# A decoder layer on one core: another timetable for the recurrence, and other memory for attention's first keys

## The chip, the core and the metric

One core of a Trainium2 chip. Its engines work beside each other, each through its own list of instructions in a fixed order: TensorE (PE; PEld is its weight load), VectorE (DVE), ScalarE (ACT), GpSimd (POOL), and SyncE (SP), which here issues the DMA transfers. They wait for each other by semaphores. The metric is the device time of one execution in microseconds, the median of several runs.

## The reference

One layer on x (1024 rows of 1024), all in float32. Cut to what matters:

```python
xn = rms_norm(x, norm_g)
z = xn @ w_in                       # q, c_kv, q_idx, k_idx, w_idx, g_attn, x_rnn, g_rnn, merge
s_idx = sum_j relu(q_idx_j @ k_idx.T) * w_idx_j        # index scores, causal
_, idx = lax.top_k(s_idx, 256)                         # for each row the 256 best keys
o = softmax(q_lat @ c_sel.T - slope * dist) @ c_sel    # attention over the chosen keys, 16 heads
y_attn = (o * silu(g_attn)) @ w_attn_proj
u = causal_depthwise_conv(x_rnn, conv_w, conv_b)
r, i = sigmoid(u_blocks @ w_a + b_a), sigmoid(u_blocks @ w_x + b_x)
a = exp(-8 * r * softplus(-lam))
h = scan(h * a + sqrt(1 - a*a) * (i * u))              # RG-LRU, along the sequence
y_rnn = (h * silu(g_rnn)) @ w_rnn_proj
g_a, g_r = split(sigmoid(merge + b_merge))
out = rms_norm(x + (g_a * y_attn + g_r * y_rnn) @ w_out, final_norm_gain)
```

## The kernel before

Each projection is made in three matmuls: both operands are split into a high and a low part (`split`, L94 to L96: the high part by ScalarE, the low part by GpSimd or VectorE), and three of the four products are added in PSUM (`proj_steps`, L116 to L124). A projection of 128 output columns for all 1024 rows is called a long piece here: 16 steps of three matmuls (L529: `step`), 512 rows wide each. Its weights come in two DMA transfers of 256 KB and are split one long piece ahead.

The stages are: normalisation and transposes; index scores; the stage of the timetable; attention with its projections; the output. The stage of the timetable holds three independent kinds of work:

- the recurrence, in four pairs of 128-channel groups c and d: input projections `xr` of c and d, convolution on VectorE (`conv`, L557 and L559), the split of its result (`both_parts`, ScalarE and GpSimd), gate projections `gr` of c and d with the small matmuls of the recurrence's gates between their steps (`gate_part`, L575 to L582); then the tail of the pair: `decay` (ScalarE), `radicand`, `root` and `scan` (VectorE), and the result is stored to DRAM (`u_r`, L608);
- the merge gates of the recurrence, `mr` 0 to 7, eight long pieces whose only consumer is the projection `rp` of the recurrence's result; then that projection, `rp` 4 to 7 and 0 to 3, whose result is multiplied by the gate on VectorE (L513) and stored (`mr_d`, L514);
- the choice of the 256 best keys, by a search for a threshold, bit by bit, 31 rounds. For the row blocks 2 to 5 (the near ones) a round is four counts and a step on VectorE (`near_round`, L633 to L647). For blocks 6 and 7 (the far ones) it is two sums of signs and a flag on ScalarE (`far_sums`, L656 to L660), and one small step on VectorE (`far_step`, L663: it writes `neg`, which the next round reads). After the rounds each block is selected in five steps (`select_at`, L729 to L742); for the far ones `far_last` (L684 to L691) comes before.

The order of all this is a timetable: every piece is entered with a time by `at_time`, the entries are sorted by it, and each engine's instructions are recorded in that order. So the times set the order alone; on the chip nothing waits for them. `STEP` is 0.68 for a step of a long piece, `LONG` 10.9.

After the pairs the recurrence's memory is closed (`close_rec`), the stored result is fetched in eight transfers of 512 KB (`fetch_u`, L759), and split (`part_u`: high part on ScalarE, low part on VectorE, for groups 2 and 5 on GpSimd), while the last merge gates run on TensorE. Then `rp` begins.

Attention opens a memory pool `at` where the stage's pools stood. A pool gives each tag its place when the first tile of it is asked for. In the kernel before the first are `vr` (the values' copy), `kh` and `kl` (keys), `qt` (queries); so `vr` stands on the memory of the products of `rp` (pool `grp`), and may be written once their stores to `mr_d` are done. The first key matmul's PSUM bank is that of the last projection's first half, which VectorE's product (L513) reads.

Of the kernel before, what the change touches and what calls it, by code (L numbers as in the profile page):

```python
# [8 lines left out]
F32 = mybir.dt.float32  # L9
F32R = mybir.dt.float32r  # L10
# [8 lines left out]
P = 128  # L19
S = 1024  # L20
# [32 lines left out]
def hybrid_kernel(ctx: ExitStack, tc: tile.TileContext, x, w_b, w_a, w_ap, w_rp, w_o, vecs,  # L53
# [98 lines left out]
    with ExitStack() as p12:  # L152
# [41 lines left out]
        with tc.tile_pool(name="xprep", bufs=3) as xp:  # L194
# [14 lines left out]
            for i in range(NB):  # L209
# [6 lines left out]
                if i < 2 or i % 2 == 0:  # L216
                    n = 1 if i < 2 else 2
# [168 lines left out]
        with tc.manual_schedule(engines={mybir.EngineType.PE}):  # L386
# [6 lines left out]
            for g in range(NG):  # L393
# [10 lines left out]
                for j in (2 * g, 2 * g + 1):  # L404
                    for cost in score_steps(j):
                        debt += cost * pace
                        while debt > 0:
                            f = next(beside, None)
# [41 lines left out]
        def at_time(t, fn, *a):  # L450
            plan.append((t, len(plan), fn, a))
# [215 lines left out]
        def near_round(t, apart=0.0):  # L667
            k = bits["near"]
            bits["near"] -= 1
            for b in near:  # L670
                at_time(t, lambda b=b: count(b, thf[:, b - B0:b - B0 + 1], ALU.is_ge))
                t += apart or 0.18 + 0.00108 * P * (b + 1)
            at_time(t, near_step, k)
            return t + 1.0

        def far_round(t):
            at_time(t, far_sums, bits["far"])
            bits["far"] -= 1
            at_time(t + 3.3, far_step)
# [96 lines left out]
        t = 0.0  # L776
        for p in range(4):
            c, d = 2 * p, 2 * p + 1
            t0 = t
            if p:  # L780
                tail(t0, c - 2, c - 1)
                near_round(t0 + 0.8)
                far_round(t0 + 15.0)
            else:
                near_round(t0 + 17.5)
            at_time(t0 + 1.0, gate_weights, c)
            at_time(t0 + 12.5, gate_weights, d)
            t = long(t, "mr", p)
            t1 = long(t, "xr", c)
            t2 = long(t1, "xr", d)  # L790
            at_time(t1 + 0.8, conv, c)
            at_time(t1 + 6.0, both_parts, c)
            near_round(t1 + 6.1)
            far_round(t1 + 2.4)
            at_time(t2 + 0.8, conv, d)
            at_time(t2 + 6.0, both_parts, d)
            near_round(t2 + 6.1)
            t3 = long(t2, "gr", c, gate_parts(c), 4)
            near_round(t3 - 1.4)
            far_round(t3 - 2.0)  # L800
            t = long(t3, "gr", d, gate_parts(d), 4)
            near_round(t - 7.5)
            far_round(t - 3.4)

        t0 = t
        tail(t0, 6, 7)
        near_round(t0 + 0.8)
        for n in range(4, 8):
            t = long(t, "mr", n)
        at_time(t0 + 23.0, close_rec)  # L810
        for c in range(8):
            at_time(t0 + 24.0, fetch_u, c)
            at_time(t0 + 29.0 + 2.0 * c, part_u, c)
        for n in (4, 5, 6, 7, 0, 1, 2, 3):
            t = long(t, "rp", n)
            if n > 3:
                at_time(t + 1.0, again, n - 4)
        for u in (15.0, 20.0, 36.2):
            far_round(t0 + u)
        u = t0 + 45.0  # L820
        while bits["far"] >= 0:
            far_round(u)
            u += 4.4
        far_end = u
        near_round(t0 + 23.2)
        for u in (28.6, 36.6):
            near_round(t0 + u, 2.0)
        u = t0 + 45.5
        while bits["near"] >= 0:
            u = near_round(u)  # L830
        at_time(t0 + 55.0, distances)
# [3 lines left out]
        for b in near:  # L835
            u = select_at(u, b)
        u = max(u, far_end)
# [3 lines left out]
        for b in FAR_B:  # L841
            u = select_at(u, b)
# [21 lines left out]

        with ExitStack() as p2:
            at = p2.enter_context(tc.tile_pool(name="at", bufs=2))
            p2.enter_context(tc.manual_schedule(engines={mybir.EngineType.PE}))
            vts, vraw, qts, khs, kls, os_, sgs, ws = {}, {}, {}, {}, {}, {}, {}, {}

# [568 lines left out]
```

## Time and profile before

| | us |
|---|---|
| median of 3 runs | 1199.71 (1199.65 to 1200.52) |
| profiled execution | 1199.43 |
| its span, first to last instruction | 1197.6 |
| TensorE busy | 1147.1 (96%) |
| VectorE busy | 847.4 (71%) |
| ScalarE busy | 752.8 (63%) |
| GpSimd busy | 475.0 (40%) |

Busy shares are means over stages that are bound differently. The stage of the timetable runs from about 153 us (first input projection) to 543 us (first key matmul of attention). On TensorE its borders are: pair 0 with its merge gate before 200.9, the three other pairs until 390.6, four merge gates until 434.2, the projection `rp` until 538. TensorE has two clock levels, 1.2 and 2.4 GHz; the windows show the granted share of the higher one, as a mean. An idle time stands in brackets with what ended it; where several semaphores are waited for, the last by the profile is named.

### The profile page before, as it was taken

To read this page: it belongs to the slowest core of one execution; us is meant where nothing else is said; L and a number is where in the kernel's file an instruction comes from. 1 tells how busy PE (TensorE), PEld (TensorE's weight loads), DVE (VectorE), ACT (ScalarE), POOL (GpSimd) and SP (SyncE) were. 2 spreads that over 40 slices of the span, in tenths; PEclk is the share of its full clock that TensorE was granted. 3 is DMA by queue.
4 is the path that set the end of the run, shared out by engine and by line. 5 is a ranking of instruction groups with operands and counts; after the bars stand their busy time and mean duration, and the time that the engine had idled before them with its cause. 6 is when DMAs were issued, how large, how long until landed. Compare 5 with 4: busy or idle time off the path is not lost.

```text
span 1197.6 us, 16198 instructions
## 1 busy us (share of the span) xinstructions
PE 1147.1 (96%) x5528; PEld 957.1 (80%) x5528; DVE 847.4 (71%) x1740; ACT 752.8 (63%) x1444; POOL 475.0 (40%) x379
## 2 busy tenths in 40 slices
PE   6989999989998979999999999999999998999997
PEld 5978888768787857877888888888888877888886
DVE  6878587888888669986867676767667699533335
ACT  6457549778787865636877767776767677322211
POOL 4211145454656342243453534344434436363000
PEclk8989999989999998999999999999999999999999
DMA  5110221313131143322011111111010241453322
GB/s 207 51 36 19 71 67 45 105 36 115 36 110 36 71 183 113 114 99 69 11 45 42 49 52 42 45 37 63 28 64 27 89 158 36 165 187 127 96 86 114
DMA packets 44402, 94.19 MB, mean 79 GB/s; under 512 B 5280, under 2 KB 8864, under 8 KB 44320
## 3 DMA queue, kind: packets, MB, share of 16 engines
q1 hardware_dynamic: 44176, 92.89, 22.8%
q8 instruction: 44, 0.72, 0.3%
q14 instruction: 38, 0.31, 0.1%
q10 hardware_dynamic: 144, 0.26, 0.1%
HBM read 70.59 MB, written 22.54 MB: 78 GB/s over the span
## 4 chain that ended last, share of the span: by engine, by line
PE 49%; DVE 2%; ACT 1%; issue 1%; DMA 1%; POOL 1%; POOLq 0%; ACTq 0%; DVEq 0%
PE pT L1273 5%; PE o L1227 3%; PE l L1069 3%; PE l L1070 2%; PE f L113 2%; PE f L114 2%; PE z_q L122 2%; PE f L112 2%; PE z_q L124 2%; PE z_q L123 2%; PE z_g L122 2%; PE z_g L124 2%; PE z_g L123 2%; PE z_ap L124 2%; PE z_ap L123 2%; PE z_ap L122 2%
## 5 line engine op out<-in xcount | busy, mean ns | idle before, releaser
L1277 DVE TENSOR_TENSOR pp<-pT,pp 128x512 fp32r<-128x512 f32 (+1 forms) x160 | 100.8, 634 | 36.7 <-ACT pp L1276 35.2
L1276 ACT ACTIVATE pp<-pT 128x512 fp32r<-128x512 f32 (+1 forms) x160 | 87.9, 551 | 52.3 <-PE pT L1273 50.3
L633 DVE TENSOR_SCALAR_CACHE_REDUCE junk<-sc,thr 128x384 bf16<-128x384 f32 (+4 forms) x130 | 106.2, 817 | 3.2
L656 ACT ACTIVATE junk<-sc,neg 128x896 int8<-128x896 f32 (+1 forms) x62 | 67.9, 1095 | 30.1 <-DVE neg L663 28.8
L1227 PE MATMUL o<-pp,vt 128*128 128x512 f32 x160 | 66.9, 418 | 2.2 <-DVE o L1242 1.0
L1069 PE MATMUL l<-kh,qt 128*128 128x128 f32 (+2 forms) x192 | 64.7, 339 | 1.6 <-DVE m L1071 0.9
L1070 PE MATMUL l<-kl,qt 128*128 128x128 f32 (+2 forms) x192 | 65.5, 342 | 0.0
L1077 ACT ACTIVATE l<-l,m 128x128 f32<-128x128 f32 (+4 forms) x80 | 54.0, 675 | 16.7 <-DVE m L1071 16.4
L1082 POOL TENSOR_SCALAR sc<-sc,m 128x384 f32<-128x384 f32 (+1 forms) x32 | 25.8, 808 | 87.8 <-DVE m L1079 79.6
L123 PE MATMUL z_rp<-url,whi_rp 128*128 128x512 f32 x128 | 52.6, 411 | 6.7 <-POOL url L96 3.5
L1242 DVE TENSOR_TENSOR o<-o,o 64x256 f32<-64x256 f32 x128 | 53.4, 419 | 6.8 <-ACT o L1240 4.6
L378 ACT ACTIVATE r<-s 128x512 f32<-128x512 f32 (+1 forms) x80 | 39.8, 522 | 26.2 <-PE s L377 23.4
L122 PE MATMUL z_q<-xh,whi_q 128*128 128x512 f32 x128 | 53.7, 419 | 0.2 <-DVE kl L953 0.2
L1077 ACT ACTIVATE sc<-sc,m 128x384 f32<-128x384 f32 (+2 forms) x48 | 44.9, 935 | 13.5 <-DVE m L1071 12.0
L383 DVE SCALAR_TENSOR_TENSOR sc<-r,wi,sc 128x384 f32<-128x384 f32 (+5 forms) x42 | 40.6, 1000 | 18.0 <-ACT r L378 17.7
L124 PE MATMUL z_rp<-urh,wlo_rp 128*128 128x512 f32 x128 | 52.1, 407 | 0.9 <-POOL wlo_rp L96 0.9
L96 POOL TENSOR_TENSOR xs<-xc,xs 64x1024 fp32r<-64x1024 f32 x16 | 38.4, 2402 | 36.2 <-ACT xs L95 28.3
L122 PE MATMUL z_rp<-urh,whi_rp 128*128 128x512 f32 x128 | 51.9, 405 | 0.6 <-ACT whi_rp L95 0.6
L122 PE MATMUL z_gr<-xh,whi_gr 128*128 128x512 f32 x128 | 51.3, 401 | 0.0
L1273 PE MATMUL pT<-ident,sc 128*128 128x128 f32 x288 | 48.9, 272 | 2.6 <-DVE pp L1277 2.6
L123 PE MATMUL z_gr<-xl,whi_gr 128*128 128x512 f32 x128 | 51.1, 399 | 0.0
L124 PE MATMUL z_gr<-xh,wlo_gr 128*128 128x512 f32 x128 | 51.0, 398 | 0.0
(356 smaller groups left out, 3921.2 us busy)
## 6 DMA issues: line engine op xcount, KB each, us to landing
xt<-in_x_dram SPq DMA_DIRECT2D x8, 512.0 KB, 8.8
wraw_mr<-in_w_b_dram SPq DMA_DIRECT2D x16, 256.0 KB, 2.7
wraw_xr<-in_w_b_dram SPq DMA_DIRECT2D x16, 256.0 KB, 2.7
wraw_gr<-in_w_b_dram SPq DMA_DIRECT2D x16, 256.0 KB, 2.7
u_r<-ig SPq DMA_DIRECT2D x8, 512.0 KB, 2.7
url<-u_r SPq DMA_DIRECT2D x8, 512.0 KB, 7.5
wraw_rp<-in_w_rp_dram SPq DMA_DIRECT2D x16, 256.0 KB, 3.1
mr_d<-grm SPq DMA_DIRECT2D x16, 256.0 KB, 2.0
```

The lines of the kernel that those rows point to most:

```text
L122: nc.tensor.matmul(acc, wh, xh_, start=(k == 0), stop=False)
L123: nc.tensor.matmul(acc, wh, xl_, start=False, stop=False)
L124: nc.tensor.matmul(acc, wl, xh_, start=False, stop=(k == KT - 1))
L633: nc.vector.tensor_scalar(junk[:, :P * (b + 1)], SL(b), thr_, None, op0=op, op1=ALU.add, accum_out=cnt[:, b - B0:b - B0 + 1])
L656: nc.scalar.activation(junk2[:, :P * (b + 1)], SL(b), AF.Sign, bias=nf[:, j:j + 1], accum_out=sums[:, j:j + 1])
L1069: nc.tensor.matmul(acc[:, :n], q, kh[:, c0:c0 + n], start=True, stop=False)
L1070: nc.tensor.matmul(acc[:, :n], q, kl[:, c0:c0 + n], start=False, stop=True)
L1077: nc.scalar.activation(l[:, :L], l[:, :L], AF.Exp, scale=-1.0, bias=mi, accum_out=m[:, 2:3])
L1227: nc.tensor.matmul(ov, vt[:, 2 * jj, :], pp[:, :, 0:256], start=(jj == 0), stop=False)
L1273: nc.tensor.transpose(tp[:, k * P:(k + 1) * P], pr[u][:, j * P:(j + 1) * P], ident)
L1276: latest[:] = [nc.scalar.activation(pp[:, 0, :n], tp[:, :n], AF.Copy), nc.vector.tensor_tensor(out=pp[:, 1, :n], in0=tp[:, :n], in1=pp[:, ...
L1277: nc.vector.tensor_tensor(out=pp[:, 1, :n], in0=tp[:, :n], in1=pp[:, 0, :n].bitcast(F32), op=ALU.subtract)]
```

## The change

The timetable is changed, and the order in which attention's memory is handed out. The merge gate that opened a pair (`mr` p in pair p) now opens the next one: pair 0 has none, pairs 1 to 3 have `mr` 0 to 2, and behind the pairs there are five (`mr` 3 to 7) in place of four. A pair has three far rounds: the one at t3 - 2.0, between the two gate projections, is gone, and pair 0's first is new at 2.0. Behind the pairs there are five fixed far rounds in place of three, and then one every 4.4 from 53.0 on in place of 45.0; the fixed near rounds are five in place of four. The splits of the fetched result stand 2.7 apart from 31.0 on, in place of 2.0 from 29.0 on. Before attention's first tile is asked for, a tile of each of six tags (`pp`, `o`, and four buffers of logits) is asked for, so that these get the lowest places.

```diff
@@ timetable of a pair
             t0 = t
+            near_round(t0 + 0.8)
             if p:
                 tail(t0, c - 2, c - 1)
-                near_round(t0 + 0.8)
-                far_round(t0 + 15.0)
-            else:
-                near_round(t0 + 17.5)
+                t = long(t, "mr", p - 1)
+            far_round(t0 + (15.0 if p else 2.0))
...
-            t = long(t, "mr", p)
...
             near_round(t3 - 1.4)
-            far_round(t3 - 2.0)
@@ behind the pairs
-        for n in range(4, 8):
+        for n in range(3, 8):
             t = long(t, "mr", n)
...
-            at_time(t0 + 29.0 + 2.0 * c, part_u, c)
+            at_time(t0 + 31.0 + 2.7 * c, part_u, c)
...
-        for u in (15.0, 20.0, 36.2):
+        for u in (15.0, 20.0, 25.0, 38.0, 46.1):
             far_round(t0 + u)
-        u = t0 + 45.0
+        u = t0 + 53.0
         while bits["far"] >= 0:
...
@@ attention
             at = p2.enter_context(tc.tile_pool(name="at", bufs=2))
+            for tag, w, dt, bufs in (("pp", S, F32R, 3), ("o", S, F32, 1), ("l0", P, F32, 1), ("l1", 2 * P, F32, 1),
+                                     ("l3", 4 * P, F32, 1), ("l4", 5 * P, F32, 1)):
+                at.tile([P, w], dt, tag=tag, name=f"{tag}_", bufs=bufs)
```

The order on ScalarE in the last pair, from the gates of group c (`r`, `ig`, read from PSUM banks `rg`) over the gate projection's second half (`sg`) and the next weights (`whi_mr`) to the first gates of group d. Before:

```order
L579 ACTIVATE r_3245<-rg_1_512_3362,vec 64x512
L579 ACTIVATE ig_3246<-rg_1_512_3362,vec 64x512
L656 ACTIVATE junk_1517,sums<-sc,neg 128x896
L656 ACTIVATE junk_1517,sums<-sc,neg 128x1024
L659 ACTIVATE sgn<-sums,lims 128x1 x2
L660 ACTIVATE flip<-sgn 128x2
L489 ACTIVATE sg_3275<-z_gr_512_3339 128x512
L95 ACTIVATE whi_mr_0_3397<-wraw_mr_0_3395 128x512
L95 ACTIVATE whi_mr_512_3403<-wraw_mr_512_3401 128x512
L579 ACTIVATE r_3334<-rg_0_0_3426,vec 64x512
L579 ACTIVATE ig_3335<-rg_0_0_3426,vec 64x512
```

and now:

```order
L579 ACTIVATE r_3166<-rg_1_0_3269,vec 64x512
L579 ACTIVATE ig_3167<-rg_1_0_3269,vec 64x512
L579 ACTIVATE r_3166<-rg_1_512_3283,vec 64x512
L579 ACTIVATE ig_3167<-rg_1_512_3283,vec 64x512
L489 ACTIVATE sg_3196<-z_gr_512_3260 128x512
L95 ACTIVATE whi_mr_0_3313<-wraw_mr_0_3311 128x512
L95 ACTIVATE whi_mr_512_3319<-wraw_mr_512_3317 128x512
L579 ACTIVATE r_3255<-rg_0_0_3341,vec 64x512
L579 ACTIVATE ig_3256<-rg_0_0_3341,vec 64x512
```

The four rows of the far round (two sums, the sign, the flag) between the gates of c and the gates of d are gone.

The order of SyncE's DMA issues at the fetch: `u_r` is the store of the recurrence's result, `url` the fetch, `wraw` the weights of the next long pieces. Before:

```order
L100 DMA wraw_mr_0_3664<-in_w_b_dram 128x512
L100 DMA wraw_mr_512_3670<-in_w_b_dram 128x512
L608 DMA u_r_80<-ig_3335 128x1024
L759 DMA url<-u_r_73 128x1024
L759 DMA url<-u_r_74 128x1024
L759 DMA url<-u_r_75 128x1024
L759 DMA url<-u_r_76 128x1024
L759 DMA url<-u_r_77 128x1024
L759 DMA url<-u_r_78 128x1024
L759 DMA url<-u_r_79 128x1024
L759 DMA url<-u_r_80 128x1024
L100 DMA wraw_rp_0_3760<-in_w_rp_dram 128x512
```

and now:

```order
L608 DMA u_r_80<-ig_3256 128x1024
L759 DMA url<-u_r_73 128x1024
L759 DMA url<-u_r_74 128x1024
L759 DMA url<-u_r_75 128x1024
L759 DMA url<-u_r_76 128x1024
L759 DMA url<-u_r_77 128x1024
L759 DMA url<-u_r_78 128x1024
L759 DMA url<-u_r_79 128x1024
L759 DMA url<-u_r_80 128x1024
L100 DMA wraw_mr_0_3679<-in_w_b_dram 128x512
L100 DMA wraw_mr_512_3685<-in_w_b_dram 128x512
L100 DMA wraw_rp_0_3766<-in_w_rp_dram 128x512
```

The weights of the last merge gate stood ahead of the fetch and now stand behind it, in the place of the first weights of `rp`.

The order on VectorE at the end of the selection of block 5 (`eq` to `sc`), with the steps of the far rounds (`neg`) and the products (`grm`), up to the first row of `far_last` (`tf`). Before:

```order
L736 SCALAR_TENSOR_TENSOR eq_4293<-pre_4294,need_4144,eq_4293 128x768
L739 SCALAR_TENSOR_TENSOR eq_4293<-sc,thr,eq_4293 128x768
L742 SCALAR_TENSOR_TENSOR sc<-eq_4293,dist 128x768
L663 TENSOR_TENSOR neg<-neg,flip 128x2
L513 TENSOR_TENSOR grm_3970<-grm_3970,z_rp_512_4309 128x512
L663 TENSOR_TENSOR neg<-neg,flip 128x2
L684 TENSOR_SCALAR tf<-neg 128x2
```

and now:

```order
L736 SCALAR_TENSOR_TENSOR eq_4244<-pre_4245,need_4113,eq_4244 128x768
L739 SCALAR_TENSOR_TENSOR eq_4244<-sc,thr,eq_4244 128x768
L663 TENSOR_TENSOR neg<-neg,flip 128x2
L742 SCALAR_TENSOR_TENSOR sc<-eq_4244,dist 128x768
L513 TENSOR_TENSOR grm_3994<-grm_3994,z_rp_0_4261 128x512
L663 TENSOR_TENSOR neg<-neg,flip 128x2
L513 TENSOR_TENSOR grm_3994<-grm_3994,z_rp_512_4311 128x512
L663 TENSOR_TENSOR neg<-neg,flip 128x2 x2
L513 TENSOR_TENSOR grm_4091<-grm_4091,z_rp_0_4344 128x512
L684 TENSOR_SCALAR tf<-neg 128x2
```

Behind the last selection row (`sc<-eq`) two steps of far rounds stood, and now three, with one more just ahead of it; one product more stands in front of `far_last`.

## Rows read from the trace of the kernel before

**Rows 1.** The page's busy shares: engine, busy us, share, instructions.
```profile
PE 1147.1 (96%) x5528; PEld 957.1 (80%) x5528; DVE 847.4 (71%) x1740; ACT 752.8 (63%) x1444; POOL 475.0 (40%) x379
```
**Rows 2.** Windows by stage: length, busy us by engine, granted clock, DMA share, GB/s.
```profile
153.07:200.90 47.83, 47.67 (x210) 39.05 (x209) 40.06 (x71) 33.05 (x55) 26.23 (x17) 1.00 0.19 63
200.90:266.60 65.70, 61.45 (x257) 49.61 (x256) 53.52 (x79) 53.42 (x88) 34.35 (x20) 0.95 0.21 68
266.60:328.94 62.34, 60.07 (x257) 49.14 (x256) 52.90 (x74) 50.08 (x81) 34.38 (x20) 0.97 0.22 72
328.94:390.56 61.62, 58.47 (x258) 47.99 (x256) 52.24 (x70) 49.47 (x77) 34.39 (x20) 1.00 0.21 71
390.56:434.20 43.64, 43.64 (x193) 35.86 (x191) 28.79 (x46) 30.25 (x48) 11.60 (x7) 1.00 0.42 157
434.20:538.00 103.80, 95.62 (x387) 73.94 (x387) 95.16 (x165) 60.27 (x129) 36.71 (x27) 0.95 0.30 101
```
**Rows 3.** Waits of TensorE: total us, times, longest.
```profile
PE rg L575 <- POOL wlo_mr L96: 8.9, 3, 3.5
```
**Rows 4.** Timeline of ScalarE, third pair: start, us, engine, line; in brackets idle before.
```profile
379.40 1.04 ACT L656 ACTIVATE junk<-sc,neg 128x896 int8<-128x896 f32 x1
...
382.21 0.20 ACT L660 ACTIVATE flip<-sgn 128x2 int32<-128x2 f32 x1
```
**Rows 5.** Timeline of VectorE, end of the last pair.
```profile
393.90 0.69 DVE L490 TENSOR_TENSOR sg<-sg,z_gr 128x512 f32<-128x512 f32 x1 [1.87 <-ACT sg L489]
```
**Rows 6.** Timeline of VectorE, GpSimd and TensorE, pair 0.
```profile
164.85 0.81 DVE L557 TENSOR_SCALAR xc<-xr,vec 128x1024 f32<-128x1024 f32 x1 [3.49 <-ACT xr L482]
...
172.69 2.39 POOL L96 TENSOR_TENSOR xs<-xc,xs 64x1024 fp32r<-64x1024 f32 x1 [3.63 <-ACT xs L95]
...
178.91 0.39 PE L575 MATMUL rg<-xs,rgh 128*128 128x512 f32 x1
```
**Rows 7.** Timeline of SyncE's DMA issues, the fetch.
```profile
419.59 4.37 SPq L759 DMA_DIRECT2D url<-u_r  x8
424.38 13.35 SPq L100 DMA_DIRECT2D wraw_rp<-in_w_rp_dram  x4
```
**Rows 8.** Timeline of ScalarE and VectorE behind the fetch.
```profile
434.15 1.27 ACT L95 ACTIVATE whi_rp<-wraw_rp 128x512 fp32r<-128x512 f32 x2 [8.32 <-DMA wraw_rp<-in_w_rp_dram]
...
437.35 3.42 DVE L96 TENSOR_TENSOR url<-url,urh 128x1024 fp32r<-128x1024 f32 x1 [7.92 <-ACT urh L95]
```
**Rows 9.** Line 656 (far rounds) in 446 to 515: durations, starts, idle before.
```profile
L656 ACT ACTIVATE junk<-sc,neg x26: 1027/1096/1151, 446.1 to 512.0; 128x896 int8<-128x896 f32 x13, 128x1024 int8<-128x1024 f32 x13
...
  DVE neg L663: 20.4, 11
```
**Rows 10.** Timeline of VectorE, the last selections.
```profile
507.69 1.01 DVE L736 SCALAR_TENSOR_TENSOR eq<-pre,need,eq 128x768 f32<-128x768 f32 x1
...
510.67 0.15 DVE L663 TENSOR_TENSOR neg<-neg,flip 128x2 int32<-128x2 int32 x1
...
513.91 0.16 DVE L663 TENSOR_TENSOR neg<-neg,flip 128x2 int32<-128x2 int32 x1 [2.49 <-ACT flip L660]
...
526.63 2.01 DVE L736 SCALAR_TENSOR_TENSOR eq<-pre,need,eq 128x896 f32<-128x896 f32 x1
...
542.25 1.28 DVE L513 TENSOR_TENSOR grm<-grm,z_rp 128x512 f32<-128x512 f32 x2
```
**Rows 11.** Timeline of TensorE, start of attention.
```profile
542.99 0.50 PE L112 MATMUL k<-cnh,ukh 128*128 128x512 f32 x1 [2.11 <-DVE grm L513]
...
557.79 0.30 PE L1069 MATMUL l<-kh,qt 128*128 128x128 f32 x1 [0.63 <-PE z_q L124]
```
**Rows 12.** Timeline of ScalarE, start of attention.
```profile
547.22 2.07 ACT L919 ACTIVATE vr<-v 128x512 f32<-128x512 f32 x4 [0.33 <-DMA mr_d<-grm]
```
**Rows 13.** Timeline of GpSimd beside the selection of block 6.
```profile
523.07 4.61 POOL L96 TENSOR_TENSOR wlo_rp<-wraw_rp,whi_rp 128x512 fp32r<-128x512 f32 x2 [3.30 <-ACT whi_rp L95]
```
**Rows 14.** The page's costliest groups, line 633 (near counts).
```profile
L633 DVE TENSOR_SCALAR_CACHE_REDUCE junk<-sc,thr 128x384 bf16<-128x384 f32 (+4 forms) x130 | 106.2, 817 | 3.2
```

More of the change, by code (lines that the diff above doesn't have):

```diff
@@ L806, in hybrid_kernel @@
         tail(t0, 6, 7)
-        near_round(t0 + 0.8)
-        for n in range(4, 8):
+        for n in range(3, 8):
             t = long(t, "mr", n)
@@ L816, in hybrid_kernel @@
             if n > 3:
-                at_time(t + 1.0, again, n - 4)
-        for u in (15.0, 20.0, 36.2):
+                at_time(t + 3.0, again, n - 4)
+        for u in (15.0, 20.0, 25.0, 38.0, 46.1):
             far_round(t0 + u)
-        u = t0 + 45.0
+        u = t0 + 53.0
         while bits["far"] >= 0:
@@ L824, in hybrid_kernel @@
         far_end = u
+        near_round(t0 + 0.8)
         near_round(t0 + 23.2)
-        for u in (28.6, 36.6):
-            near_round(t0 + u, 2.0)
-        u = t0 + 45.5
+        for u in (31.5, 39.6, 47.7):
+            near_round(t0 + u, 1.95)
+        u = t0 + 55.8
         while bits["near"] >= 0:
```

## The prediction

> **What bounds the kernel now.** First the page's busy shares: TensorE works 96% of the span [rows 1], so a change pays only where TensorE stands still, or where its clock falls. Second the windows, cut at the stage borders that TensorE's own rows give [rows 2]. In the three stretches 200.90 to 390.56 (a pair each) TensorE idles 4.25, 2.27 and 3.15 us, and in 434.20 to 538.00 (the recurrence's projection) 8.18. The clock column says more: a mean clock of 0.95, 0.97 and 0.95 over 65.70, 62.34 and 103.80 us is a loss of 3.3, 1.9 and 5.2 us, since a stretch at 1.2 GHz does half the work. With the 2.11 us in front of the first key matmul [rows 11] the idle is 20.0 and the clock loss some 12 with what follows that wait. Third the list of waits: the stalls in the pairs are the gate matmuls' [rows 3], put down to GpSimd, but GpSimd had long been done. In the third pair ScalarE runs a far round from 379.40 to 382.41 [rows 4] ahead of the copies that free the gates' PSUM banks, and only then can TensorE go on. Fourth VectorE: in 434.20 to 538.00 it is busy 95.16 of 103.80 us [rows 2], from 513.91 on it works through the last two selections and the last products until 542.9 [rows 10], and the first key matmul waits for its last product [rows 11]. So TensorE and VectorE reach attention nearly together, and what is saved on TensorE alone stops at VectorE.
>
> **The change, part by part.** I follow VectorE, since its last product releases the keys.
>
> *Pair 0 without its merge gate.* Four gates are the 192 matmuls of the window from 390.56, 43.64 us, so one is 10.9 [rows 2]. TensorE passes it on to the tail, where the total is the same. VectorE's first convolution waited 3.49 us for the recurrence's input, until 164.85 [rows 6]; that input is now made a gate earlier, so the wait goes. ScalarE's first far round (3.0 us, as in rows 4) now stands before the copy and takes about 0.5 back: VectorE gains 3.0. TensorE arrives much earlier and meets a new wait: in before the GpSimd split for the first gate matmul ended 10.2 us after the convolution began (172.69 + 2.39 - 164.85 [rows 6]); the convolution now begins at about 161.9, so the split is there at 172.1, and TensorE at 178.91 - 10.9 = 168.0: a wait of 4.1, and some 2 of lost clock, as after the 2.27 us wait [rows 2]. It costs the end nothing as long as VectorE comes later than TensorE.
>
> *One far round fewer in each pair.* The round of rows 4 goes, 3.0 us of ScalarE, four times. TensorE's waits of 3.45, 2.27 and 3.15 shrink to about 0.4, 0 and 0.1. VectorE waits for ScalarE at the pair's end (1.87 [rows 5]) and in the tail of the recurrence. It gains between 1.87 and 3.0 a pair; I take 2.5. Its busy time in the three later pairs is 53.52, 52.90 and 52.24 [rows 2], its idle time in an ordinary one 9.4; with 6.9 they last 60.4, 59.8 and 59.1, together 179.3 against 189.7: 10.4 earlier. Pair 0 gives 3.0 + 2.5. VectorE is then 15.9 us earlier at the end of the pairs.
>
> *Five gates beside the fetch.* The recurrence's result is fetched in eight transfers from 419.59; the next weights are issued behind them at 424.38 [rows 7] and ScalarE waits 8.32 us for them, until 434.15; VectorE waits 7.92 us behind ScalarE [rows 8]. TensorE's 8.18 us come from there. Now a gate's weights stand in that place, and TensorE has one gate more to do before it needs the splits. So most of the 8.18, and the 5.2 of clock, go. ScalarE and VectorE, however, wait just as before. What is late next is the order behind the wait. VectorE has two counts more there (2 x 0.82 [rows 14]), one split more (between 0 and the 3.42 of rows 8; I take half, 1.7), one product less (0.64), and the wait ends 1.0 sooner, as one 128x1024 copy less stands in front: +1.7.
>
> *Three far rounds more behind the pairs.* From 446.1 to 513.9 thirteen rounds took 67.8 us, 5.2 each; ScalarE needs 3.0 and waited 20.4 us for VectorE in that time [rows 9], so as long as VectorE has other work, a further round is hidden. It is not hidden after the fourth near block's selection. There the order shows one flag that is waited for before and three now; each costs 513.91 - 510.67 = 3.24 [rows 10], and between the last two ScalarE also splits a pair of weights (1.27, as in rows 8). The first runs beside one more selection step (1.01 [rows 10]). 3 x 3.24 + 1.27 - 1.01 = 10.0 against 3.24: +6.8. Bounds: 0, if ScalarE gets ahead in time; 15.6, if each of three costs the full 5.2.
>
> *The last two selections.* The weights of the last projection are issued earlier against the last flag, since the product in front of them moved ahead. The selection step at 526.63 took 2.01 for 896 columns, the one at 507.69 took 1.01 for 768 [rows 10], and beside the slow one GpSimd split weights from 523.07 to 527.68 [rows 13]. The Trainium skill (SBUF — State Buffer, section "Who interferes with whom") has it that a VectorE instruction with two SBUF inputs and a GpSimd instruction that reads SBUF block each other for the whole instruction; these rows agree. By that rule the doubling moves with the splits rather than with the selection, and all six slow steps could lose it, or other work could gain it. From the rows alone: two steps lose 1.0 each: -2.0, with 0 and -5.5 as bounds (five or six slowed steps of about 1.0).
>
> *Attention's first keys in other memory.* The values' copy stood on the memory of the products and waited for their stores (547.22, released by mr_d [rows 12]); the changed order of allocation puts it on the fetched result's memory, which the last projection matmul frees. On TensorE this wait is worth no more than the 0.63 us before the first logits at 557.79 [rows 11], because 48 query matmuls (10.9 us) lie beside it. -0.6. If it added a wait instead, the same 10.9 us would hide it.
>
> *Sum.* VectorE's last product, and with it the first key matmul, comes 15.9 - 1.7 - 6.8 + 2.0 = 9.4 us earlier. TensorE, with its waits and lost clock gone (20.0 + 12, less 6 new in pair 0 and the 1.9 behind the key matmul's own wait), would be there 24 us earlier, so for some 15 us in all it waits there and for the last projections' weights, which are issued behind the stores of products. A longer wait costs more clock: after the wait of 2.11 it was about as much as the 1.9 of the second window; I take 3.3 as in the first [rows 2], +1.4, less 0.6 for the keys: +0.8. Profiled execution: 1199.43 - 9.4 + 0.8 = 1190.8 (the span of 1197.6 and the 1.8 around it, which does not change). The median of the runs is 0.28 above that execution: 1191.1.
>
> **The rivals.**
> 1. *TensorE sets the pace.* VectorE and the far chain keep up, because VectorE's idle time in the pairs (9.4 to 12.2 each) is enough to take in everything. Then all 20.0 of idle and 12 of clock go, less 6 new in pair 0: 1199.7 - 26 = 1173.5, and what lies between that and my forecast. For it: no single row shows VectorE out of reach. Against it: 95.16 of 103.80 busy, and three serial flags.
> 2. *No change.* VectorE's waits in the pairs stay at 9.4 each (only the longer first one falls to that): 186.8 instead of 189.7 in three pairs, 2.9, and 3.0 in pair 0. Then 5.9 - 8.5 + 2.0 = -0.6, and 1199.43 + 0.6 + 0.8 + 0.28 = 1201.1. For it: the other waits there are for ScalarE's chain behind a table load, which does not change.
> 3. *Slower: VectorE's order paces both stages.* Pairs as in 2, and the three moved rounds pass at the 5.2 of rows 9 instead of filling gaps: 15.6 for 6.8, and the 1.7 stays. -5.9 + 15.6 + 1.7 - 2.0 + 0.8 = +10.2: 1210. Place: 446 to 514 of the trace; it decides once a pair still lasts 61.6 or more and the last flag comes more than 134 us after the last gate projection (123 now). Against it: ScalarE's 20.4 us of waiting.
> 4. *The memory alone works* and the timetable cancels out: 0.6, within what can be told.
>
> **How the numbers follow.** My forecast (1187 to 1197.2) has 0.53, rival 1 (1173 to 1187) 0.24, rivals 2 and 4 (1197.3 to 1202) 0.14, rival 3 0.09. The bounds of the unknown terms move it: with the flags hidden and all slow selections cured, 1191.1 - 6.8 - 3.5 = 1181; with 1.87 a pair, no cured selection and a full split, 1191.1 + 2.5 + 2.0 + 1.7 = 1197.3. The range runs from 1180 to 1199, which leaves out most of rival 3, half of rival 2 and the far part of rival 1. About 0.2% (2.4 us) is what a measurement tells from no change: faster 0.77, within 0.14, slower 0.09.
>
> **What would show it.** Right: pairs of 59 to 60.5 us without waits of the gate matmuls in the third quarter; a wait of 3 to 5 us at the very first gate matmul; no idle TensorE at the start of the recurrence's projection beyond 2 to 4 us, but VectorE waiting 7 to 11 us for ScalarE there; three flags of 3.2 us after the fourth selection; the first key matmul near 533 after a wait of 5 us or more for VectorE; values copied at once. Wrong: a key matmul that does not wait (rival 1), pairs of 62 us (rivals 2 and 3), flags that VectorE waits for all along the projection (rival 3).

## The result and the profile after

The changed kernel takes 1187.44 us in the median of four runs (1184.53 to 1187.90), against 1199.68 of the kernel before beside it: a ratio of 0.9893, with an interval of 0.9876 to 0.9911. In a second comparison, the first experiment below, it was 1186.67 us and 0.9888 (0.9873 to 0.9903). The forecast was 1191.1 in a range of 1180 to 1199, so the time lies inside, 3.7 us under the forecast. Two profiles of the changed kernel exist, of executions of 1184.53 and 1189.02 us, and the difference between these two is the most instructive part of the result.

First the busy shares of the first of them, and its windows, cut at the same borders on TensorE as before (pair 0, three pairs, five gates, the projection). Pair 0 now begins at 131.31, since no gate stands in it; it begins among the last matmuls of the stage before, so its 63.44 us can't be set beside the 47.83 of [rows 2].

```profile
PE 1139.1 (96%) x5528; PEld 951.9 (81%) x5528; DVE 847.0 (72%) x1740; ACT 751.4 (64%) x1444; POOL 474.8 (40%) x379
```

```profile
131.31:194.75 63.44, 59.10 (x256) 48.39 (x255) 48.78 (x79) 39.42 (x69) 28.81 (x25) 0.95 0.15 48
194.75:254.13 59.38, 58.67 (x257) 47.81 (x256) 54.07 (x70) 47.21 (x72) 34.37 (x20) 1.00 0.23 76
254.13:314.42 60.29, 58.92 (x257) 47.82 (x256) 54.86 (x74) 48.15 (x75) 34.32 (x20) 1.00 0.23 75
314.42:374.70 60.28, 58.87 (x257) 47.81 (x256) 54.83 (x74) 48.15 (x75) 33.74 (x20) 1.00 0.21 72
374.70:431.12 56.42, 54.97 (x241) 44.89 (x240) 40.13 (x66) 44.38 (x74) 20.35 (x12) 1.00 0.39 143
431.12:527.66 96.54, 92.09 (x387) 73.13 (x386) 83.98 (x160) 56.69 (x128) 30.20 (x25) 0.98 0.33 110
```

Against [rows 2]: the pairs last 59.4, 60.3 and 60.3 us in place of 65.7, 62.3 and 61.6, at the full clock, and TensorE idles 0.7 to 1.4 us in each. The projection lasts 96.5 us in place of 103.8. TensorE did the same 5528 matmuls in 8 us less busy time; it spent some 17 us less at the 1.2 GHz level, half of which is lost.

Not all of the first profile's gain belongs to the change. The windows 62 to 82 us, in the index scores, where both kernels are the same, show the kernel before with a mean clock of 0.74 and the changed one with 0.83:

```profile
62.00:82.00 20.00, 15.17 (x66) 13.45 (x65) 13.62 (x23) 9.49 (x19) 3.13 (x3) 0.74 0.09 27
```

```profile
62.00:82.00 20.00, 14.91 (x73) 13.17 (x73) 14.80 (x24) 10.64 (x21) 4.26 (x3) 0.83 0.09 27
```

From there on every matmul of the first profile is 1.5 us earlier, 1.2 us in the second one. This is chance, and I take it off below: the stretch at half clock in the index scores lasts 10.2 us in five of the thirteen profiles of this document and 6.8 us in the other eight, with kernels of both timetables in either group.

In pair 0 the new wait of the first gate matmul is there, and behind the pairs the wait for the weights behind the fetch. The columns are start, length, engine, line, and in brackets the idle time before; SPq is SyncE's queue. TensorE:

```profile
171.03 0.80 PE L575 MATMUL rg<-xs,rgh 128*128 128x512 f32 x1 [4.33 <-POOL xs L96]
```

SyncE's issues of the fetch and of the last gate's weights:

```profile
403.79 3.85 SPq L759 DMA_DIRECT2D url<-u_r  x8
407.75 1.43 SPq L100 DMA_DIRECT2D wraw_mr<-in_w_b_dram  x2
```

VectorE, from the wait behind the fetch over the last flags to the last two products:

```profile
420.76 2.08 DVE L96 TENSOR_TENSOR url<-url,urh 128x1024 fp32r<-128x1024 f32 x1 [7.94 <-ACT urh L95]
...
493.41 1.23 DVE L663 TENSOR_TENSOR neg<-neg,flip 128x2 int32<-128x2 int32 x1
494.56 0.94 DVE L742 SCALAR_TENSOR_TENSOR sc<-eq,dist 128x768 f16<-128x768 f32 x1
...
497.72 0.16 DVE L663 TENSOR_TENSOR neg<-neg,flip 128x2 int32<-128x2 int32 x1 [1.62 <-ACT flip L660]
...
500.96 0.16 DVE L663 TENSOR_TENSOR neg<-neg,flip 128x2 int32<-128x2 int32 x1 [2.48 <-ACT flip L660]
504.91 0.16 DVE L663 TENSOR_TENSOR neg<-neg,flip 128x2 int32<-128x2 int32 x1 [3.79 <-ACT flip L660]
...
529.14 1.28 DVE L513 TENSOR_TENSOR grm<-grm,z_rp 128x512 f32<-128x512 f32 x2
```

The wait of 7.94 is that of [rows 8], and the three flags behind the selection of block 5 take 11.5 us from the step at 493.41, where [rows 10] had one of 3.24. The last product ends at 530.42, 13.1 us before that of [rows 10].

The first key matmul starts at 530.37 and waits for nothing: TensorE and VectorE arrive together. In the second profile they do not. TensorE of the second profile, then its window behind that wait (length, busy times, clock), and the window of the same length and place of the first profile:

```profile
532.11 0.80 PE L112 MATMUL k<-cnh,ukh 128*128 128x512 f32 x1 [3.22 <-DVE grm L513]
```

```profile
532.10:539.00 6.90, 6.89 (x18) 5.50 (x19) 1.50 (x3) 3.90 (x9) 3.68 (x5) 0.56 0.25 87
```

```profile
530.37:537.00 6.63, 6.63 (x32) 5.48 (x31) 1.24 (x4) 4.16 (x10) 3.94 (x6) 1.00 0.26 90
```

A wait of 3.22 us, and behind it TensorE works at 0.56 of the full clock; in the first profile no wait and 1.00. From the first key matmul to the first logits it takes 15.2 us there and 13.3 here (14.8 in the kernel before; 0.8 of the 13.3 and 0.6 of the 14.8 are a wait in front of the logits). So the changed kernel sits at a tie between two engines: which comes last is decided by small things, and the wait of the one that comes first can cost the clock as well. Its executions lie from 1184.5 to 1189.0. The tie need not be the whole reason for that spread: the fourth far round below, in whose profile VectorE is not the last, has executions from 1181.5 to 1186.6.

Of the memory part the profile shows that nothing changed. ScalarE's copy of the values, in the first profile:

```profile
532.84 2.07 ACT L921 ACTIVATE vr<-v 128x512 f32<-128x512 f32 x4 [4.69 <-DMA ukr<-in_w_uk_dram]
```

It starts 2.5 us behind the first key matmul, right after the two last stores of products (issued at 529.85 and 530.45, 2.1 us to landing), as it did in [rows 12]. The bracket names another DMA, which landed at that moment; in ten of the profiles the copy starts 0.2 to 0.3 us behind the landing of the last store, whichever DMA the bracket names.

### The profile page after: what moved, and what is told of

It reads as the page before. It is cut to its first block, busy times and chain, and to the rows that moved or that the text cites. A ratio compares the mean times of both kernels' runs of the same rounds, so it can differ in the third digit from the quotient of the medians.

```text
span 1182.4 us, 16202 instructions
## 1 busy us (share of the span) xinstructions
PE 1139.1 (96%) x5528; PEld 951.9 (81%) x5528; DVE 847.0 (72%) x1740; ACT 751.4 (64%) x1444; POOL 474.8 (40%) x379
## 4 chain that ended last, share of the span: by engine, by line
PE 61%; DVE 15%; ACT 13%; issue 5%; DMA 3%; POOL 2%; SPq 0%; POOLq 0%; ACTq 0%; DVEq 0%
PE pT L1275 5%; DVE xc L559 3%; DVE junk L633 3%; PE o L1229 3%; PE l L1071 3%; PE l L1072 2%; PE f L114 2%; PE f L112 2%; PE f L113 2%; PE z_q L122 2%; PE z_q L124 2%; PE z_q L123 2%; PE z_g L122 2%; PE z_g L124 2%; PE z_g L123 2%
## 5 line engine op out<-in xcount | busy, mean ns | idle before, releaser
L1081 DVE RECIPROCAL m<-m 128x1 f32<-128x1 f32 x128 | 20.4, 159 | 42.4 <-ACT l L1079 23.0
L122 PE MATMUL z_mr<-xh,whi_mr 128*128 128x512 f32 x128 | 49.9, 390 | 0.8 <-ACT whi_mr L95 0.8
L124 PE MATMUL z_mr<-xh,wlo_mr 128*128 128x512 f32 x128 | 49.9, 390 | 0.6 <-POOL wlo_mr L96 0.6
```

The lines of the kernel that those rows point to most:

```text
L122: nc.tensor.matmul(acc, wh, xh_, start=(k == 0), stop=False)
L124: nc.tensor.matmul(acc, wl, xh_, start=False, stop=(k == KT - 1))
```

## The experiments

Theory A, the prediction's: VectorE's last product decides when attention begins, and the far rounds decide VectorE's. Theory B: TensorE's own stalls decide, above all the one before the projection. Ratios are against the kernel before, run on the same chip. The last seven experiments ran on other chips than the changed kernel's 1186.67 us, so their differences to it are good to about 1 us; where the ratios say something else, that is given.

**The changed kernel again.** Nothing is edited.

> The changed kernel once more, beside the others on one chip. In its first profile VectorE's last product ended just as TensorE was ready for the first key matmul, so the two bounds lie within 1 us. That execution took 1184.5 us, the three others 1187.1 to 1187.9. Theory A (a tie of the two engines, and chance decides which comes last): the median is 1186 to 1188, and a second profile shows either a wait of up to 1 us at the first key matmul, or half-clock stretches at other places than the first. Theory B (the first profile was the odd one out by 1.5 us in the index scores, where it spent one half-clock stretch of 6.8 instead of 10.2 us before the change begins): the second profile has the long stretch there, and the rest is the same as in the first.

Measured: 1186.67 us, 0.9888 (0.9873 to 0.9903). The profiled execution, 1189.02 us, spent the same half-clock stretch in the index scores as the first (the matmuls there are 0.3 us apart), so B falls; what differs is the tie, so theory A, though with 3.2 us of waiting instead of "up to 1". TensorE was 1.6 us earlier in this profile, since the stretch at a mean clock of 0.66 that the first profile has from 492 to 497 is not there:

```profile
492.00:497.00 5.00, 4.28 (x12) 3.40 (x13) 4.10 (x4) 2.30 (x5) 2.62 (x2) 0.66 0.52 172
```

And VectorE was 2.2 us later (the section on the hardware says why). TensorE, earlier, then waited longer and lost more: the execution with the slower TensorE ended 4.5 us sooner.

**The memory part alone.**

```diff
  at = p2.enter_context(tc.tile_pool(name="at", bufs=2))
+ for tag, w, dt, bufs in (("pp", S, F32R, 3), ("o", S, F32, 1), ... ):
+     at.tile([P, w], dt, tag=tag, name=f"{tag}_", bufs=bufs)
```

> The kernel before with the memory part alone: six tags of attention asked for first. The prediction gave this part 0.6 us, from a values' copy that no longer waits for the products' stores. The profile after contradicts the mechanism: the values' copy still starts only when the last store has landed. So theory A (prediction): the copy starts at once and the time is 0.6 lower. Theory B: the copy waits as before, the time is the same within 0.5 us. Theory C: the move helps at another place, the idle 3.0 us of TensorE near the end of attention (1007 to 1015), which was 1.9 us after the change: 1.1 us lower, with that idle time gone.

Measured: 1199.24 us, ratio 1.0000 (0.9991 to 1.0008). Theory B of the three; the part's 0.6 us are not there. The copy still waits for the stores:

```profile
546.35 2.07 ACT L922 ACTIVATE vr<-v 128x512 f32<-128x512 f32 x4 [0.32 <-DMA mr_d<-grm]
```

The copy's wait is not for the bytes under it alone. That the closing of the pools brings it is a reading of the code, not shown.

**The timetable alone.** The changed kernel without those lines.

> The changed kernel without the memory part, so the timetable alone. By the prediction it carries the whole gain but 0.6 us: ratio 0.9895 to 0.992 against the kernel before (1187.5 to 1190). If the memory part helps near the end of attention, this kernel has about 3 us of TensorE idle there and is 1.1 us slower than the changed one; if it does nothing, the two are equal within 0.5 us.

Measured: 1186.41 us, 0.9890 (0.9877 to 0.9904), equal to the changed kernel. The 1.9 us idle near the end of attention are there without the memory part too (0.38, 0.23 and 1.31), so theory C is dead as well. Its profile is a third throw of the tie: 1.59 us of waiting at the first key matmul, then the full clock, 13.6 us to the first logits.

**The far round put back between the gate projections.**

```diff
              near_round(t3 - 1.4)
+             if p:
+                 far_round(t3 - 2.0)
```

> The changed kernel with the far round between the two gate projections put back in the last three pairs, so that three far rounds fewer stand behind the pairs. Theory A (the prediction: the far rounds' place is worth their time): the gate matmuls wait 2.3 to 3.5 us again in each of these pairs, a pair lasts 62 instead of 60.2, and VectorE leaves the pairs 6 to 9 us later; behind them two of the three serial flags vanish (6.5 us back). TensorE loses 6 to 9 us, the time is 1191 to 1196. Theory B (only the five gates beside the fetch matter): waits of the pairs are made up for by the shorter tail, and the time is within 1.5 us of the changed kernel.

Measured: 1192.65 us, 0.9942 (0.9930 to 0.9955), 6.0 us over the changed kernel: theory A. TensorE's list of waits has the old row of [rows 3] again:

```profile
PE rg L575 <- POOL wlo_mr L96: 9.2, 3, 3.5
```

Counted from the first input projection, VectorE leaves the pairs 8.9 us later than in the changed kernel and yet has its last flag 3.8 us earlier, since three rounds fewer stand behind the pairs. That gives nothing back: TensorE is now the last (no wait at the first key matmul).

**The far round taken out of the kernel before.**

```diff
-            far_round(t3 - 2.0)
+            if not p:
+                far_round(t3 - 2.0)
```

> The kernel before with one thing of the change alone: the far round between the two gate projections is taken out of the last three pairs, so that three far rounds more stand behind the pairs; the gates stay where they were. Theory A (VectorE's last product sets the first key matmul): the gate matmuls' waits go and VectorE leaves the pairs 8 to 9 us earlier, but five steps of far rounds instead of two now stand behind the last near selection, 3.2 us each and 1.3 for a split of weights between them: 10 to 11 us later. TensorE's stall at the start of the projection stays at 8. The time is that of before or up to 4 us more (1199 to 1204), with TensorE waiting 6 to 10 us for VectorE at the first key matmul. Theory B (TensorE's own stalls set it): the 6 to 9 us of the gate matmuls' waits are gained, 1191 to 1194.

Measured: 1196.09 us, 0.9971 (0.9961 to 0.9980). Between the two theories, and so a miss for both in size. Counted from the first input projection, VectorE did leave the pairs 8.8 us earlier and had its last flag 6.7 later. But while it waited for flags TensorE went on, and the products moved ahead of the selections. So VectorE's lateness no longer held the first key matmul (0.89 us) but the first logits: ScalarE's copy of the values, and behind it both parts of the keys, come after VectorE's last selection row (`sc`, L742). VectorE at the last flags, ScalarE and VectorE behind the last selection, and TensorE at the first logits, whose row names no releaser:

```profile
512.93 0.16 DVE L663 TENSOR_TENSOR neg<-neg,flip 128x2 int32<-128x2 int32 x1 [7.44 <-ACT flip L660]
...
516.17 0.16 DVE L663 TENSOR_TENSOR neg<-neg,flip 128x2 int32<-128x2 int32 x1 [2.49 <-ACT flip L660]
...
520.13 0.16 DVE L663 TENSOR_TENSOR neg<-neg,flip 128x2 int32<-128x2 int32 x1 [3.09 <-ACT flip L660]
```

```profile
544.30 2.06 ACT L920 ACTIVATE vr<-v 128x512 f32<-128x512 f32 x4 [0.24 <-DVE sc L742]
```

```profile
546.91 0.68 DVE L954 TENSOR_TENSOR kl<-k,kh 64x512 fp32r<-64x512 f32 x1 [2.64 <-ACT kh L953]
```

```profile
553.36 0.44 PE L1070 MATMUL l<-kh,qt 128*128 128x128 f32 x1 [7.08 <-issue]
```

With the experiment before it this is a square: neither part 1199, the removed rounds alone 1196, the rest of the timetable alone (the gates, with pair 0 and the times behind the pairs) 1193, both 1187. Against the runs of before beside them the two gain 2.8 and 6.9 us alone and 12.9 together: each alone stops at what the other takes away.

**The tail's far rounds closer together.**

```diff
-            u += 4.4
+            u += 3.8
```

> The changed kernel with the far rounds behind 53.0 entered 3.8 apart instead of 4.4, so that two steps stand behind the last near selection and none just ahead of it, where the changed kernel has three and one. Theory A (VectorE sets the first key matmul, and the serial flags set VectorE): its last product comes 3 to 5 us earlier, TensorE's wait of 3.2 us at the first key matmul and the half-clock stretch of 6.8 us behind it (worth 3.4) are gone: 1180 to 1184. Theory B (the chain of far rounds takes its time wherever its steps stand): VectorE waits as much more in front of the earlier steps, its last product does not move, 1186 to 1188.

Measured: 1189.08 us, 0.9917 (0.9904 to 0.9931), 2.4 us worse than the changed kernel, 3.5 by the ratios. VectorE's waits for flags behind 425 us fell from 9.1 to 5.6, and the last flag came 2.4 to 2.7 us earlier, counted from the first input projection. But the last product came only 1.6 us earlier than in the second profile of the changed kernel and 0.3 later than in the first. And ScalarE's far rounds now stood ahead of two splits of weights; TensorE's waits behind 425:

```profile
PE z_rp L122 <- ACT whi_rp L95: 3.1, 2, 1.7
PE z_rp L124 <- POOL wlo_rp L96: 2.0, 3, 1.0
PE z_rp L123 <- DVE url L96: 1.7, 1, 1.7
```

They were 2.0, 0.7 and 1.7. So neither theory is right: VectorE's flags did gain, its last product at most half of what A wanted, and TensorE, which does not wait for VectorE at the first key matmul here, lost 2.4 us in these waits by what stands behind a far round on ScalarE, which I had not counted.

**The last gate's weights on a queue of their own.** GpSimd issues the two transfers; they no longer stand behind the fetch.

```diff
+            if (kind, c) == ("mr", 7):
...
+                    nc.gpsimd.dma_start(raw, src[:, k:k + 512])
```

> The changed kernel with the weights of the last merge gate (mr 7) fetched through GpSimd's queue instead of behind the eight transfers on SyncE's. Theory A (ScalarE and VectorE lose their 8 us there to the queue): ScalarE's wait of 7.7 us for these weights falls to 1 to 4, VectorE's 7.9 likewise, VectorE's last product comes 2 to 6 us earlier, and the wait at the first key matmul goes: 1180 to 1185. Theory B (the transfers share the same DMA engines, so the fetch ends 2 us later and the splits with it): ScalarE waits for the fetch in place of the weights, 1186 to 1189.

Measured: 1183.12 us, 0.9866 (0.9853 to 0.9880), 3.5 us under the changed kernel, 2.6 by the ratios. ScalarE's wait for these weights, 7.70 us in the changed kernel, is 3.90 (and 0.64 for the second half), VectorE's 7.94 is 4.78, and its last product comes 2.0 and 3.9 us earlier than in the two profiles above, counted in the same way:

```profile
416.39 0.63 ACT L95 ACTIVATE whi_mr<-wraw_mr 128x512 fp32r<-128x512 f32 x1 [3.90 <-DMA wraw_mr<-in_w_b_dram]
```

Theory A by the time and by the waits of ScalarE and VectorE, at its small end; but the key matmul, whose wait was to go, still waits 1.49. GpSimd issues the weights no sooner behind the start of the fetch than SyncE did (4.1 us against 4.0), so what differs is the queue. So the wait that the change left in place for ScalarE and VectorE was worth something.

**Both of these.**

> Both of the two kernels before it together. If VectorE alone sets the first key matmul, the gains add up until TensorE is the last: TensorE has 3.2 us of waiting there, 3.4 of clock behind it and 2.3 in front of the recurrence's projection to give, so no less than 1178. Theory A: 1178 to 1182, no wait at the first key matmul. Theory B: no better than the better of the two, within 1 us.

Measured: 1187.65 us, 0.9903 (0.9888 to 0.9918): worse than the own queue alone, which neither theory foresaw. The closer far rounds cost TensorE the same splits of weights here, and though no wait stands at the first key matmul, TensorE waits 3.0 us in front of the first logits.

**A fourth far round a pair at another place.**

```diff
             far_round(t1 + 2.4)
+            if p:
+                far_round(t2 + 1.0)
```

> The changed kernel with a fourth far round in each of the last three pairs, as in the kernel before, but at another place: right behind the copy of group d's input projection, 3 us before the first gates, in place of the one between the two gate projections. Three rounds fewer stand behind the pairs, and no step of a far round behind the last near selection. Theory A (what hurt in the kernel before was the place between the gate projections, not the round in the pair): pairs stay at 59.5 to 61, VectorE's last product comes 5 to 9 us earlier than in the changed kernel, TensorE's wait at the first key matmul goes, and TensorE sets the time: 1182 to 1185. Theory B (ScalarE's three us are paid in the pair wherever they stand): pairs of 62, as with the round at its old place, and 1190 to 1194.

Measured: 1184.02 us, 0.9866 (0.9843 to 0.9889). Theory A: the first of the three pairs lasts 59.3 us (its gate starts at 195.22, the next pair's at 254.56), VectorE leaves the pairs at the same time as in the changed kernel, and the last flag comes at 494.17 in place of 504.91. Now VectorE waits for TensorE; its list of waits behind 425:

```profile
DVE grm L513 <- PE z_rp L124: 4.7, 1, 4.7
DVE url L96 <- ACT urh L95: 2.5, 2, 1.4
DVE neg L663 <- ACT flip L660: 1.2, 1, 1.2
```

So it was the place between the gate projections that hurt, not the round. And of the 10.7 us by which the flags came earlier, only some 2.7 reach the end: then TensorE is the last. With four executions from 1181.5 to 1186.6 these 2.7 us stand at the edge of what can be told; that the round costs nothing here, in place of the 6.0 above, does not.

**The fourth round and the own queue.**

> The same, with the weights of the last merge gate on GpSimd's queue as well. If TensorE sets the time in both, the queue adds only TensorE's own stall in front of the recurrence's projection, 1.7 to 2.3 us: 1180 to 1183, and no wait at the first key matmul. If VectorE still sets it, the queue's 3.5 us come on top as they did on the changed kernel: 1178.5 to 1181.5, with a wait there.

Measured: 1181.90 us, 0.9852 (0.9837 to 0.9867), no wait at the first key matmul: the first of the two.

**The last far round behind the weights.** As the one before, and

```diff
-            u += 4.4
+            u += 4.55
```

> The kernel before this one (four far rounds a pair, own queue) with the far rounds behind 53.0 entered 4.55 apart instead of 4.4, so that ScalarE's last far round stands behind the split of the next weights and not ahead of it. TensorE waited 2.1 and 0.7 us for that split, and its clock was at 1.2 GHz for 3.4 us right behind. Theory A (TensorE sets the time): both waits go and the stretch with them, 2.8 to 4.5 us: 1177.5 to 1179.5. Theory B (VectorE was only 0 to 2 us behind, and its last flag now comes later): TensorE waits for its last product instead, 1180.5 to 1183.

Measured: 1180.27 us, 0.9841 (0.9827 to 0.9854), the fastest of all, 0.5% under the changed kernel. Theory A in kind, not in size. ScalarE's split is in time, but GpSimd's half of it still holds TensorE, and the stretch at the lower clock behind it stays:

```profile
PE z_rp L124 <- POOL wlo_rp L96: 1.8, 1, 1.8
```

## Why the prediction was right, point by point

The shifts are those of VectorE's rows from before to after, with the chance of the index scores (1.5 us in the first profile, 1.2 in the second) taken off where a total stands.

| term, us | forecast | measured |
|---|---|---|
| pair 0 (to its tail's scans) | -5.5 | -5.6 |
| three later pairs | -10.4 | -8.8 |
| the order behind the fetch | +1.7 | -0.2 |
| selections of the near blocks | 0 | -1.2 |
| serial flags | +6.8 | +8.3 |
| last two selections | -2.0 | -4.1 first, -1.8 second profile |
| VectorE's last product | -9.4 | -11.6 first, -9.7 second |
| from the first key matmul to the end | +0.8 | -2.6 first, +0.2 second |

- *The number* owes something to luck. The sum for VectorE came out within 0.3 us in the second profile because the errors of its terms, +1.6 in the pairs and some -2 from the fetch to the last flag, cancel. In the first profile not VectorE but TensorE, 9.0 us earlier, sets the first key matmul; that this lies beside the 9.4 forecast for VectorE is luck.
- *Pair 0* came out to 0.1 us, the first gate matmul's wait too (4.1 forecast, 4.33 measured, [rows 6] against the row above). The lost clock around it is the 0.95 of 63.44 us, 3.2 for my 2. As forecast it costs the end nothing where VectorE comes later.
- *One far round fewer in each pair* is the largest term, and right in kind: the putting back costs 6.0 us of time. The size was a little high, since two of the three pairs last 60.3.
- *Five gates beside the fetch.* TensorE's 8.18 us and the clock lost behind them went; 1.73 of idle time is left at the projection's start, and 1.45 stands in front of the last gate, which I had not listed. VectorE waits 7.94 as forecast (7 to 11). The +1.7 that I charged for the order behind the wait was wrong: two more counts and a split found room in waits that VectorE has there anyway.
- *Three far rounds more behind the pairs*: three serial flags, 4.3, 3.2 and 4.0 us, as counted; a split of weights stood in front of the last, as counted. 8.3 for 6.8, but the 6.8 had 1.01 taken off for the last near selection step, which now stands behind the first flag's step and makes most of the -1.2 in the row above; like for like it is 7.3. The rest: the step at 493.41 itself took 1.23 us in place of 0.16, and the last flag 4.0 where 4.5 were counted.
- *The last two selections*: the range was right and the single value is a throw, -4.1 and -1.8 in two executions of one program.
- *The memory part* failed in its mechanism. I put it down to bytes: other memory, no wait. The copy's wait stayed, and alone the part is worth 0.0 (within 0.1%); its -0.6 in the sum is shown by no run.
- *TensorE's lead* failed in size. I had TensorE ready some 15 us ahead of VectorE, waiting 5 us or more at the first key matmul and the rest for weights. In the second profile, that of the timetable alone and the first it waits 3.2, 1.6 and 0 us there and 5 to 6 us for splits and weights in front of it. It was ready for that matmul 9.0 us earlier in the first profile and 10.8 in the second, chance taken off, where I had 24. What TensorE was to gain (20 of idle, 12 of clock), it gave back in part in waits that I had not listed, for ScalarE's far rounds ahead of the weights' splits, and in the first profile by another stretch at 1.2 GHz: of 28 us of idle time and lost clock in the stage 19 are still there in that profile, 7.7 in pair 0 (6 forecast), 3.5 in the pairs and 7.6 behind them. So rival 1, TensorE as the last, was nearer than I wrote: a key matmul that does not wait, the prediction's own sign of being wrong, stands in one of these three profiles, and in every kernel above that relieved VectorE except the own queue alone. Rival 1's time (1173.5) did not come: TensorE did not gain what it was to gain.

That the median lies 3.7 us under the forecast has these parts in the profiles: 1.2 to 1.5 of chance (whether the medians have it too is not shown), the 1.9 us wrongly charged behind the fetch, and the executions in which the tie falls TensorE's way, where the clock is not lost behind the first key matmul. How often each way occurs can't be read from a profile of one execution, and stays open.

## What to carry to other kernels

Where two engines reach a hand-over together, work out both arrivals and expect the gain of a change to stop at the second: here the two parts gave 2.8 and 6.9 us alone and 12.9 together, and of a last flag 10.7 us earlier only 2.7 came through. Before moving a chain's step on an in-order engine, list what stands behind it there (the copies that free PSUM banks, the splits of the next weights) and put the step where nothing is due, as the fourth far round showed, which cost 6 us at one place of a pair and nothing at another. A transfer whose consumer is due soon should not stand in a queue behind a bulk fetch.

## What the runs showed of the hardware

*A VectorE step that begins while a GpSimd instruction runs is longer by what that instruction has left.* In the thirteen profiles I compared the 390 selection steps of VectorE with GpSimd's instructions. Of 283 that began while none ran, none was longer than the fastest of its kind by more than 0.02 us, though in 54 of them a GpSimd instruction began before the step's end. 73 began with 0.4 to 1.2 us of a GpSimd instruction left (13 steps of a kind that was never seen undisturbed are left out): each was longer by what was left, less 0.12 to 0.21 us, for example 0.4 with 0.6 left, 0.7 with 0.9 and 1.0 with 1.1. Of the other 21, with under 0.2 left, two met the next split at once and were 1.1 longer, the others none. So the 0.9 us that are common among the slowed steps are no price of their own, and the prediction's "double" was a coincidence of size. Who begins first wins. The scan of 896 columns in the first profile began ahead of GpSimd's split, in the second one 0.6 us behind its start; VectorE and GpSimd of the first, then of the second:

```profile
513.56 2.02 DVE L732 TENSOR_TENSOR_SCAN pre<-ones,eq 128x896 f32<-128x896 f32 x1
```

```profile
514.36 2.31 POOL L96 TENSOR_TENSOR wlo_q<-wraw_q,whi_q 128x512 fp32r<-128x512 f32 x1 [2.13 <-ACT whi_q L95]
```

```profile
514.85 3.00 DVE L732 TENSOR_TENSOR_SCAN pre<-ones,eq 128x896 f32<-128x896 f32 x1
```

```profile
514.25 4.68 POOL L96 TENSOR_TENSOR wlo_q<-wraw_q,whi_q 128x512 fp32r<-128x512 f32 x2 [2.11 <-ACT whi_q L95]
```

The Trainium skill (SBUF — State Buffer, section "Who interferes with whom") has the two block each other for the whole of an instruction; these rows agree, and the loser's price is the rest of the other's instruction, within 0.2 us.

*A wait can cost most of its own length again in clock.* Behind the first key matmul the same six key and 48 query matmuls follow. Until the first logits it took 13.3 and 13.6 us behind waits of 0 and 1.59 us, 14.8 behind 2.11 and 15.2 behind 3.22, with mean clocks of 1.00, 1.00, 0.75 and 0.56 over the 6.6 to 6.9 us behind. In the first three 0.8, 1.1 and 0.6 us of it are a wait in front of the logits; without it the work took 12.4, 12.5, 14.2 and 15.2 us. Not every wait does it: the same two waits of TensorE at 491 us, 2.0 and 0.7, were followed by 1.2 GHz in the first profile and by the full clock in the second. The row of the 0.75 is the kernel before:

```profile
542.99:549.89 6.90, 6.90 (x23) 5.51 (x24) 0.59 (x2) 3.09 (x8) 2.54 (x3) 0.75 0.32 106
```
